# One hybrid decoder block on one core: the convolution's five VectorE operations three pieces apart and earlier, the merge's steps further apart, and decay's exponentials of odd chunks read straight from the running sums

## The chip, the cores and the metric

The kernel runs on one core of a Trainium2 chip as one launch. The metric is device time in microseconds (us), the median of several runs. A profiled execution gives the trace: PE is TensorE (PEld its weight loads), DVE is VectorE, ACT is ScalarE, POOL is GpSimd, SP is the engine that issues most DMAs. "L902" is line 902 of the kernel before.

## The reference, cut to what matters

```
proj = einsum('bsd,de->bse', rmsnorm(x), w_in)
(q, k, v, g_out, gk_low, gate_b, gate_c, xc, merge_a, merge_b) = split(proj)
log_g = log_sigmoid(gk_low @ w_gk_up + b_gk_up) / 16
bcum = cumsum(log_g, within chunks of 64 tokens)
q_dec, k_dec = q * exp(bcum), k * exp(-bcum)       # gated linear attention
o = rmsnorm(attention(q_dec, k_dec, v), gla_norm_w)
y_a = o * silu(g_out)
y_b = gate_b * causal_depthwise_conv(gate_c * xc, conv_w)   # three taps
merged = sigmoid(merge_a) * y_a + sigmoid(merge_b) * y_b
h = x + merged @ w_out
h = h + (silu(gate) * up) @ w_down                 # gate, up = rmsnorm(h) @ w_gate_up
return rmsnorm(h, final_norm_w)
```

There are 256 tokens, a model width of 2048, four heads and float32 throughout.

## The kernel before, in words

Every weight is streamed once, as 696 pieces of 128 x 1024 float32 (512 KB). The order of the pieces is a list written out ahead (`stream_list`). For each piece SP issues a DMA into `raw`, ScalarE makes a rounded copy `hi` (L238) and VectorE the rest `lo = raw - hi` (L243); TensorE then runs three matmuls for each product (L347 to L349). A whole product of four blocks ("eights") uses 12 matmuls of 512 columns for a piece. Some pairs of blocks (`gc`/`xc`, the gate and the input of the convolution) are computed as seven block products instead of eight ("sevens", 6 matmuls for a piece); they cost extra VectorE sums of whole pieces (L259 and L265, into the tiles `raw` and `x`).

The time of the program's own bookkeeping is the tick: one tick for each piece that TensorE uses up. `later(n, f)` puts `f` into the program n ticks on, `one_at_a_time(n, f)` at least n ticks on and two ticks after the one before. Pieces are prepared up to five ahead of TensorE (`LOOK`, and five buffers each for `raw` and `lo`). Instructions of each engine run in the order in which they stand on it; `pin` keeps some in the order of the program, the others may be moved by a scheduler. An engine that waits holds up all that stands behind on it.

The change touches two places.

**Decay.** `tables_within` builds an exponent table `eq` (128 x 8 x 256, four chunks of 64): chunks 0 and 2 get a difference (L750), chunks 1 and 3 a copy of the sums `bc` (L751). `exponential` (L738) makes two exponentials of it on ScalarE, `ek` and `eq`. `tables_across` does a similar thing on GpSimd for two more tables.

**Convolution and merge.** The gates come in four blocks i of 512 columns. When both `gc` and `xc` of block i are done, L954 multiplies them into `u`, and `conv(i)` one tick later shifts `u` by one and two tokens with six DMAs from GpSimd's queue (L889 to L894, into `u1` and `u2`; the taps were loaded long before). Five operations follow on VectorE (L902), pinned: `u1*tap1`, `u2*tap0`, `u*tap2`, `u1+u2`, `u+u1`, from tick `CONV_AT` = 12 on, one each tick. The first needs the three shifts into `u1`, the last of which is L893. `merge(i)` multiplies `u` into the gate (L907), adds `ya` a tick later (L908), and from three ticks on two sets of four transposes (`trb`, L595) go through TensorE, each of which ScalarE and VectorE copy out (L597, L598). Blocks 0, 1 and 2 run while the next pair's sevens are being multiplied; block 3 runs beside whole products only.

Of the kernel before, what the change touches and what calls it, by code (L numbers as in the profile page):

```python
# [11 lines left out]
AF = mybir.ActivationFunctionType  # L12
ALU = mybir.AluOpType
AX = mybir.AxisListType

P = 128
# [7 lines left out]
C = 64  # L24
# [160 lines left out]
def block_kernel(ctx, tc, x, xt, cols_in, gkw_in, gku_in, gnw, conv_w, finw, w_in, w_out, w_gu, w_dn, out):  # L185
    nc = tc.nc
    pin = tc.keep_in_program_order
# [11 lines left out]
    def bank(shape, name, tag=None):  # L199

        if tag is None:
            tag = f"b{turn['b'] % turn['of']}"
            turn["b"] += 1
        return psum.tile(shape, F32, tag=tag, name=name)
# [19 lines left out]
    count = {"loaded": 0, "used": 0, "tick": 0}  # L224
# [88 lines left out]
    def later(delay, fn):  # L313

        pending.append((count["tick"] + delay, fn))
# [15 lines left out]
    def one_at_a_time(delay, fn):  # L331

        spaced.append((count["tick"] + delay, fn))
# [256 lines left out]
    def transpose_block(src, t, hi, lo):  # L590

        lent.append(lent.pop(0))
        ps = bank([P, 4, P], "trb", lent[-1])
        for j in range(4):
            nc.tensor.transpose(out=ps[:, j, :], in_=src[:, j * P:(j + 1) * P], identity=ident)  # L595
        ts = slice(t * P, (t + 1) * P)
        nc.scalar.copy(hi[:, :, ts], ps)  # L597
        nc.vector.tensor_tensor(out=lo[:, :, ts], in0=ps, in1=hi[:, :, ts].bitcast(F32), op=ALU.subtract)  # L598
# [116 lines left out]
    inv = 1.0 / 16.0  # L715

    def ch(n):
        return bc[:, :, n * C:(n + 1) * C]

    def last(n):  # L720
        return bc[:, :, (n + 1) * C - 1:(n + 1) * C].to_broadcast([P, NM, C])
# [13 lines left out]

    first_exp = []

    def exponential(out, scale):  # L738

        ins = nc.scalar.activation(out, eq, AF.Exp, scale=scale)  # L740
        pin(ins)
        first_exp.append(ins.ins)

    def tables_within():
        nonlocal eq, ek
        eq = gpool.tile([P, NM, T], F32, tag="eq", name="eq")
        ek = gpool.tile([P, NM, T], F32, tag="ek", name="ek")

        for n in (0, 2):
            nc.vector.tensor_tensor(out=eq[:, :, n * C:(n + 1) * C], in0=ch(n), in1=last(n), op=ALU.subtract)  # L750
            nc.vector.tensor_copy(eq[:, :, (n + 1) * C:(n + 2) * C], ch(n + 1))  # L751
        exponential(ek, -inv)

    across = {}
# [1 line left out]
    def tables_across():  # L756

        exk = across["k"] = gpool.tile([P, NM, P], F32, tag="exk", name="exk")
        exq = across["q"] = gpool.tile([P, NM, P], F32, tag="exq", name="exq")
        nc.gpsimd.tensor_tensor(out=exk[:, :, 0:C], in0=last(0), in1=ch(0), op=ALU.subtract)  # L760
        nc.gpsimd.tensor_tensor(out=exk[:, :, 0:C], in0=exk[:, :, 0:C], in1=last(1), op=ALU.add)
        nc.gpsimd.tensor_tensor(out=exk[:, :, C:P], in0=last(1), in1=ch(1), op=ALU.subtract)
        nc.gpsimd.tensor_copy(exq[:, :, 0:C], ch(2))
        nc.gpsimd.tensor_tensor(out=exq[:, :, C:P], in0=ch(3), in1=last(2), op=ALU.add)
        with tc.issue_after(first_exp[-1]):
            nc.scalar.activation(exk, exk, AF.Exp, scale=inv)
            nc.scalar.activation(exq, exq, AF.Exp, scale=inv)

    def at(tick, fn):
        later(tick - count["tick"], fn)  # L770
# [6 lines left out]
    at(20, lambda: sum_decay(0))  # L777
    at(21, lambda: sum_decay(4))
    at(22, tables_within)
    at(23, lambda: exponential(eq, inv))  # L780
    at(25, tables_across)
    v_first = mm_first(gk_chunks, scale_rows)

# [42 lines left out]
    o = [omain.tile([P, NT, DV], F32, tag=f"m{i}", name="o") for i in range(H)]  # L826
# [51 lines left out]
    mh, ml = [None] * 4, [None] * 4  # L878
    us, ya, sb, merge_at = {}, {}, {}, {}

    def conv(i):
        u = us[i]
        u1 = ew.tile([P, NT, 512], F32, tag="u1", name="u1")
        u2 = ew.tile([P, NT, 512], F32, tag="u2", name="u2")
        taps = ew.tile([P, 3, 512], F32, tag="taps", name="taps")
        nc.gpsimd.dma_start(taps, conv_w[:, :, i * 512:(i + 1) * 512].to_broadcast([P, 3, 512]))
        nc.gpsimd.memset(u1[0:1, 0, :], 0.0)
        nc.gpsimd.memset(u2[0:2, 0, :], 0.0)
        nc.gpsimd.dma_start(u1[1:113, :, :], u[0:112, :, :])  # L889
        nc.gpsimd.dma_start(u2[2:114, :, :], u[0:112, :, :])  # L890
        nc.gpsimd.dma_start(u1[113:128, :, :], u[112:127, :, :])
        nc.gpsimd.dma_start(u2[114:128, :, :], u[112:126, :, :])
        nc.gpsimd.dma_start(u1[0:1, 1, :], u[127:128, 0, :])  # L893
        nc.gpsimd.dma_start(u2[0:2, 1, :], u[126:128, 0, :])  # L894

        def taps_of(j):
            return taps[:, j:j + 1, :].to_broadcast([P, NT, 512])

        for n, (dst, src, by, op) in enumerate(((u1, u1, 1, ALU.mult), (u2, u2, 0, ALU.mult), (u, u, 2, ALU.mult),
                                                (u1, u1, u2, ALU.add), (u, u, u1, ALU.add))):  # L900
            by = taps_of(by) if isinstance(by, int) else by
            later(CONV_AT + n, lambda d=dst, s=src, y=by, o=op: pin(nc.vector.tensor_tensor(out=d, in0=s, in1=y, op=o)))  # L902

    def merge(i, ts):

        v = sb[i][:, ts, :]
        pin(nc.vector.tensor_tensor(out=v, in0=v, in1=us[i][:, ts, :], op=ALU.mult))  # L907
        later(1, lambda: pin(nc.vector.tensor_tensor(out=v, in0=v, in1=ya[i][:, ts, :], op=ALU.add)))  # L908
        if mh[i] is None:
            mh[i] = omain.tile([P, 4, T], F32R, tag=f"m{i}", name="mh")  # L910
            ml[i] = oside.tile([P, 4, T], F32R, tag=f"m{i}", name="ml")
        for t in range(ts.start, ts.stop):
            one_at_a_time(3, lambda t=t: transpose_block(sb[i][:, t, :], t, mh[i], ml[i]))

    def gated(dst, ps):

# [4 lines left out]
    def gate(key):  # L921
        i = int(key[-1])

        def done(ps):
            if key[:-1] == "g":
                ya[i] = ew.tile([P, NT, 512], F32, tag=f"ya{i % 2}", name="ya")
                for t in range(NT):
                    nc.scalar.activation(ya[i][:, t, :], ps[t], AF.Silu, scale=r1[:, t:t + 1])
                nc.vector.tensor_tensor(out=ya[i], in0=ya[i], in1=o[i], op=ALU.mult)
            elif key[:-1] == "gb":  # L930
                sb[i] = ew.tile([P, NT, 512], F32, tag="sb", name="sb")
                for t in range(NT):
                    nc.scalar.activation(sb[i][:, t, :], ps[t], AF.Copy, scale=r1[:, t:t + 1])
            elif key[:-1] == "ma":
                gated(ya[i], ps)
            else:
                gated(sb[i], ps)

                at(max(count["tick"] + 1, merge_at.get(i, 0)), lambda: merge(i, slice(0, NT)))

        return done

    def gate_pair(pair):
        i = int(pair[0][-1])

        def second(t):
            to = us if pair[0][:-1] == "gc" else sb
            if i not in to:
                to[i] = ew.tile([P, NT, 512], F32, tag="u" if to is us else "sb", name="u" if to is us else "sb")
            return to[i][:, t, :]  # L950

        def done(t, one, two):
            if pair[0][:-1] == "gc":
                nc.vector.scalar_tensor_tensor(out=two, in0=one, scalar=r1sq[:, t:t + 1], in1=two,  # L954
                                               op0=ALU.mult, op1=ALU.mult)
                if t == 0:
                    later(1, lambda: conv(i))
                    merge_at[i] = count["tick"] + CONV_AT + 7
            else:
                nc.scalar.activation(two, two, AF.Sigmoid, scale=r1[:, t:t + 1])  # L960
                nc.vector.scalar_tensor_tensor(out=two, in0=one, scalar=r1[:, t:t + 1], in1=two,
                                               op0=ALU.mult, op1=ALU.mult)

                later(3 if t else 1, lambda: merge(i, slice(t, t + 1)))

        return second, done
# [191 lines left out]
    for e in order:  # L1158
        key, k0 = e
        n = int(key.split("_")[1])  # L1160
# [18 lines left out]
    assert not pending and not spaced and not ready and count["loaded"] == len(stream) + 1  # L1179


CONV_AT = 12
X_AT = (50, 54, 58, 62)
H_AT = (2, 4, 6, 8)
SQ_AT = (5, 7, 9, 11)
# [55 lines left out]
```

## Time and profile before

| what | value |
|---|---|
| median of 3 runs | 1503.78 us (1503.6, 1503.78, 1507.01) |
| the profiled execution | 1504.81 us, of which the span of its instructions is 1503.1 us |
| TensorE busy | 1489.7 us, 99% of the span, 7064 matmuls |
| VectorE busy | 1277.8 us, 85% |
| ScalarE busy | 864.1 us, 57% |
| granted TensorE clock | 0.999 of full speed |

A matmul of 512 columns is listed with 0.39 us because its end is modelled; the next one starts 0.23 us after it when nothing is waited for. So a wait of TensorE is read from the start of one matmul to the start of the next, less 0.227 us; the idle time that a row lists is 0.16 us shorter.

### The profile page before, as it was taken

The numbers are of one execution on the slowest core, as the hardware profiler recorded it, in microseconds if no ns is written. First come the engines' busy times: TensorE is split into PE (matmuls) and PEld (weight loads), VectorE is DVE, ScalarE is ACT, GpSimd is POOL, SyncE is SP. The second block draws the span as 40 slices with busy tenths as digits, with TensorE's granted clock in tenths as the row PEclk, the third lists the DMA queues.
The fourth block names the chain that finished last, engine by engine and source line by source line (L and its number), as shares of the span: only waits on it lengthen the run. The fifth ranks groups of instructions, "written<-read, shape, count | busy, mean of one in ns | idle before, by whom it ended". The sixth has DMA issues, their size and how long they took to land.

```text
span 1503.1 us, 19370 instructions
## 1 busy us (share of the span) xinstructions
PE 1489.7 (99%) x7064; PEld 1244.8 (83%) x7064; DVE 1277.8 (85%) x1283; ACT 864.1 (57%) x977; POOL 38.0 (3%) x60
## 2 busy tenths in 40 slices
PE   9999999999999999999999999999999999999997
PEld 8989988888887888888888888888888788888887
DVE  6785868979979878966689999999999999999975
ACT  7773546655655655654566755655565556565553
POOL 0030000000000000000000000000000000000000
PEclk9999999999999999999999999999999999999999
DMA  9656557876876878787677777776877788787782
GB/s 349 201 172 174 177 166 251 288 225 234 285 259 232 297 237 257 249 258 215 209 221 219 238 253 251 250 253 218 275 242 239 259 255 277 242 264 234 231 297 90
DMA packets 100128, 358.58 MB, mean 239 GB/s; under 512 B 11492, under 2 KB 11620, under 8 KB 99904
## 3 DMA queue, kind: packets, MB, share of 16 engines
q1 hardware_dynamic: 96656, 346.73, 70.8%
q0 software_dynamic: 2800, 8.89, 2.2%
q10 hardware_dynamic: 576, 1.72, 0.3%
q8 instruction: 55, 0.90, 0.2%
q14 instruction: 41, 0.34, 0.1%
HBM read 351.03 MB, written 2.10 MB: 235 GB/s over the span
## 4 chain that ended last, share of the span: by engine, by line
PE 53%; DVE 1%; issue 0%; ACT 0%; DVEq 0%; ACTq 0%
PE fg L347 8%; PE fg L349 8%; PE fg L348 8%; PE dn L347 5%; PE dn L349 5%; PE dn L348 5%; PE wo L347 2%; PE wo L348 2%; PE wo L349 2%; PE fu L349 1%; PE fu L347 1%; PE fu L348 1%; PE trb L595 1%; PE mb L349 0%; PE mb L348 0%
## 5 line engine op out<-in xcount | busy, mean ns | idle before, releaser
L243 DVE TENSOR_TENSOR lo<-raw,hi 128x1024 fp32r<-128x1024 f32 (+1 forms) x506 | 612.0, 1217 | 110.9 <-ACT hi L238 27.9
L238 ACT CAST hi<-raw 128x1024 fp32r<-128x1024 f32 (+1 forms) x506 | 523.9, 1047 | 269.9 <-PE gb L349 27.7
L238 ACT CAST hi<-x 128x1024 fp32r<-128x1024 f32 x144 | 151.7, 1053 | 267.4 <-DVE x L265 207.1
L243 DVE TENSOR_TENSOR lo<-x,hi 128x1024 fp32r<-128x1024 f32 x144 | 176.1, 1223 | 37.5 <-ACT hi L238 26.6
L347 PE MATMUL dn<-lo,acth 128*128 128x512 f32 (+1 forms) x368 | 140.7, 382 | 1.7 <-DVE h L1098 0.9
L349 PE MATMUL dn<-hi,acth 128*128 128x512 f32 (+1 forms) x368 | 139.9, 380 | 0.0
L348 PE MATMUL dn<-hi,actl 128*128 128x512 f32 (+1 forms) x368 | 139.9, 380 | 0.0
L265 DVE TENSOR_TENSOR x<-x,raw 128x1024 f32<-128x1024 f32 x96 | 117.0, 1218 | 12.0 <-DMA raw<-in_w_in_dram 7.7
L347 PE MATMUL fg<-lo,hh 128*128 128x512 f32 x288 | 112.4, 390 | 0.0
L349 PE MATMUL fg<-hi,hh 128*128 128x512 f32 x288 | 112.2, 390 | 0.0
L348 PE MATMUL fg<-hi,hl 128*128 128x512 f32 x288 | 112.2, 389 | 0.0
L347 PE MATMUL fg<-lo,sh 128*128 128x512 f32 x256 | 101.0, 395 | 0.0
L348 PE MATMUL fg<-hi,sl 128*128 128x512 f32 x256 | 99.9, 390 | 0.0
L349 PE MATMUL fg<-hi,sh 128*128 128x512 f32 x256 | 99.8, 390 | 0.0
L347 PEld LDWEIGHTS dn<-lo,acth 128*128 128x128 f32 x368 | 69.2, 188 | 15.8 <-DVE h L1098 1.8
L349 PEld LDWEIGHTS dn<-hi,acth 128*128 128x128 f32 x368 | 69.2, 188 | 13.3
L348 PEld LDWEIGHTS dn<-hi,actl 128*128 128x128 f32 x368 | 69.2, 188 | 12.9
L347 PEld LDWEIGHTS fg<-lo,hh 128*128 128x128 f32 x288 | 54.1, 188 | 11.8 <-DVE lo L243 0.5
L349 PEld LDWEIGHTS fg<-hi,hh 128*128 128x128 f32 x288 | 54.1, 188 | 11.3
L348 PEld LDWEIGHTS fg<-hi,hl 128*128 128x128 f32 x288 | 54.1, 188 | 11.0
L243 DVE TENSOR_TENSOR lo<-y,hi 128x1024 fp32r<-128x1024 f32 x48 | 58.5, 1218 | 4.8 <-ACT hi L238 2.1
L259 DVE TENSOR_TENSOR raw<-y,x 128x1024 f32<-128x1024 f32 x48 | 58.5, 1219 | 4.2 <-DMA y<-in_w_in_dram 3.3
(247 smaller groups left out, 3070.1 us busy)
## 6 DMA issues: line engine op xcount, KB each, us to landing
raw<-in_w_in_dram SPq DMA_DIRECT2D x254, 512.0 KB, 4.5
raw<-in_w_gu_dram SPq DMA_DIRECT2D x176, 512.0 KB, 4.4
raw<-in_w_dn_dram SPq DMA_DIRECT2D x88, 512.0 KB, 4.5
x<-in_w_gu_dram SPq DMA_DIRECT2D x32, 512.0 KB, 4.8
y<-in_w_gu_dram SPq DMA_DIRECT2D x32, 512.0 KB, 3.9
raw<-in_w_out_dram SPq DMA_DIRECT2D x32, 512.0 KB, 4.3
y<-in_w_in_dram SPq DMA_DIRECT2D x16, 512.0 KB, 4.4
x<-in_w_in_dram SPq DMA_DIRECT2D x16, 512.0 KB, 4.8
```

The source lines that it names most:

```text
L238: nc.scalar.copy(hi[:, ks, :], raw[:, ks, :])
L243: nc.vector.tensor_tensor(out=lo[:, ks, :], in0=raw[:, ks, :], in1=hi[:, ks, :].bitcast(F32), op=ALU.subtract)
L259: nc.vector.tensor_tensor(out=raw, in0=y, in1=held["x"], op=ALU.add)
L265: nc.vector.tensor_tensor(out=x, in0=x, in1=other, op=ALU.add)
L347: nc.tensor.matmul(ps, lhsT=sh, rhs=ml, start=first, stop=False, skip_group_check=onto)
L348: nc.tensor.matmul(ps, lhsT=sl, rhs=mh, start=False, stop=False, skip_group_check=onto)
L349: nc.tensor.matmul(ps, lhsT=sh, rhs=mh, start=False, stop=last, skip_group_check=onto)
L595: nc.tensor.transpose(out=ps[:, j, :], in_=src[:, j * P:(j + 1) * P], identity=ident)
```

## The change

The odd chunks are no longer copied into `eq` (two VectorE copies less) or `exq` (one GpSimd copy less); ScalarE reads them straight from `bc`, so two exponentials of 2048 elements become four of 1024, and one of 1024 becomes two of 512. The convolution's operations stand at ticks 6, 9, 12, 15, 18 for blocks 0 to 2 and 6, 8, 10, 12, 14 for block 3, in place of 12 to 16. The merge may begin 21 ticks (block 3: 17) after the point from which it was 19; its addition comes two ticks after its product, not one; the transposes come at least four ticks after, not three.

```diff
-        ins = nc.scalar.activation(out, eq, AF.Exp, scale=scale)
-        pin(ins)
+        for o, i in zip(halves(out), (halves(eq)[0], halves(bc)[1])):
+            ins = nc.scalar.activation(o, i, AF.Exp, scale=scale)
+            pin(ins)
...
             nc.vector.tensor_tensor(out=eq[:, :, n * C:(n + 1) * C], in0=ch(n), in1=last(n), op=ALU.subtract)
-            nc.vector.tensor_copy(eq[:, :, (n + 1) * C:(n + 2) * C], ch(n + 1))
...
-        nc.gpsimd.tensor_copy(exq[:, :, 0:C], ch(2))
...
-            nc.scalar.activation(exq, exq, AF.Exp, scale=inv)
+            nc.scalar.activation(exq[:, :, 0:C], ch(2), AF.Exp, scale=inv)
+            nc.scalar.activation(exq[:, :, C:P], exq[:, :, C:P], AF.Exp, scale=inv)
...
-            later(CONV_AT + n, lambda d=dst, s=src, y=by, o=op: pin(nc.vector.tensor_tensor(out=d, in0=s, in1=y, op=o)))
+            later(CONV_AT[i] + CONV_STEP[i] * n, lambda d=dst, s=src, y=by, o=op: pin(nc.vector.tensor_tensor(out=d, in0=s, in1=y, op=o)))
...
-        later(1, lambda: pin(nc.vector.tensor_tensor(out=v, in0=v, in1=ya[i][:, ts, :], op=ALU.add)))
+        later(2, lambda: pin(nc.vector.tensor_tensor(out=v, in0=v, in1=ya[i][:, ts, :], op=ALU.add)))
...
-            one_at_a_time(3, lambda t=t: transpose_block(sb[i][:, t, :], t, mh[i], ml[i]))
+            one_at_a_time(4, lambda t=t: transpose_block(sb[i][:, t, :], t, mh[i], ml[i]))
...
-                    merge_at[i] = count["tick"] + CONV_AT + 7
+                    merge_at[i] = count["tick"] + CONV_AT[i] + 4 * CONV_STEP[i] + 3
...
-CONV_AT = 12
+CONV_AT = (6, 6, 6, 6)
+CONV_STEP = (3, 3, 3, 2)
```

The order of instructions moves in three places that matter. Line numbers in the new kernel are 5 higher here: its L907 is the old L902 (convolution), its L912 and L913 the old L907 and L908 (merge), its L924 the old L919 (the sigmoid's product); in `lo<-raw,hi` and `lo<-x,hi` stand the pieces' splits.

**VectorE, block 1, the start of the convolution.** `u_3961` is the once shifted `u1`. Before, from the split of the piece `y` on:

```order
L243 TENSOR_TENSOR lo<-y,hi 128x1024
L265 TENSOR_TENSOR x<-x,raw 128x1024
L243 TENSOR_TENSOR lo<-raw,hi 128x1024 x2
L243 TENSOR_TENSOR lo<-x,hi 128x1024
L265 TENSOR_TENSOR x<-x,y 128x1024
L243 TENSOR_TENSOR lo<-raw,hi 128x1024
L243 TENSOR_TENSOR lo<-x,hi 128x1024
L902 TENSOR_TENSOR u_3961<-u_3961,taps 128x1024
```

Now, from the same split on:

```order
L243 TENSOR_TENSOR lo<-y,hi 128x1024
L907 TENSOR_TENSOR u_3961<-u_3961,taps 128x1024
L243 TENSOR_TENSOR lo<-raw,hi 128x1024
L265 TENSOR_TENSOR x<-x,raw 128x1024
L243 TENSOR_TENSOR lo<-raw,hi 128x1024
L907 TENSOR_TENSOR u_3962<-u_3962,taps 128x1024
L243 TENSOR_TENSOR lo<-x,hi 128x1024
L265 TENSOR_TENSOR x<-x,y 128x1024
```

The first operation on the shifted data stands seven instructions earlier, right behind that split. In block 0 it stands just ahead of the split of `y`, six splits earlier than before; in block 2 just ahead of a split of `x`, six splits earlier.

**VectorE, block 1, the merge.** `sb` is the gate that becomes the merged block. Before:

```order
L919 TENSOR_TENSOR sb<-sb,mb_0_4024 128x512
L919 TENSOR_TENSOR sb<-sb,mb_1_4025 128x512
L243 TENSOR_TENSOR lo<-x,hi 128x1024
L907 TENSOR_TENSOR sb<-sb,u 128x1024
L265 TENSOR_TENSOR x<-x,y 128x1024
L243 TENSOR_TENSOR lo<-raw,hi 128x1024
L908 TENSOR_TENSOR sb<-sb,ya 128x1024
L243 TENSOR_TENSOR lo<-x,hi 128x1024
L243 TENSOR_TENSOR lo<-raw,hi 128x1024
L265 TENSOR_TENSOR x<-x,raw 128x1024
```

Now:

```order
L243 TENSOR_TENSOR lo<-x,hi 128x1024
L924 TENSOR_TENSOR sb<-sb,mb_0_4024 128x512
L265 TENSOR_TENSOR x<-x,y 128x1024
L924 TENSOR_TENSOR sb<-sb,mb_1_4025 128x512
L243 TENSOR_TENSOR lo<-raw,hi 128x1024
L912 TENSOR_TENSOR sb<-sb,u 128x1024
L243 TENSOR_TENSOR lo<-x,hi 128x1024
L243 TENSOR_TENSOR lo<-raw,hi 128x1024
L265 TENSOR_TENSOR x<-x,raw 128x1024
L913 TENSOR_TENSOR sb<-sb,ya 128x1024
```

The addition of `ya`, for which the transposes wait, now stands behind three more instructions of the stream (two splits and a sum), and the product with `u` behind the split of `raw` that it stood ahead of. Block 0 moves in the same way; in block 2 this stretch stands as before.

**TensorE, block 1, the first set of transposes.** `g_0` and `g_1` are the two token halves of one piece of the gate `g`. Before, the transposes stand four matmuls into the piece:

```order
L349 MATMUL gc_3_3997<-hi,sh 128x512
L347 MATMUL g_0_4309<-lo,xh 128x512
L348 MATMUL g_0_4309<-hi,xl 128x512
L349 MATMUL g_0_4309<-hi,xh 128x512
L347 MATMUL g_0_4309<-lo,xh 128x512
L595 MATMUL trb<-ident,sb 128x128 x4
L348 MATMUL g_0_4309<-hi,xl 128x512
```

Now they stand at its end, after all twelve, and the next `gc` piece follows:

```order
L349 MATMUL g_0_4308<-hi,xh 128x512
L347 MATMUL g_1_4309<-lo,xh 128x512
L348 MATMUL g_1_4309<-hi,xl 128x512
L349 MATMUL g_1_4309<-hi,xh 128x512
L347 MATMUL g_1_4309<-lo,xh 128x512
L348 MATMUL g_1_4309<-hi,xl 128x512
L349 MATMUL g_1_4309<-hi,xh 128x512
L595 MATMUL trb<-ident,sb 128x128 x4
L347 MATMUL gc_2_3996<-lo,sh 128x512
```

So the transposes moved back by eight matmuls. In block 2 they moved by the same eight; in block 0 by 21, from five matmuls into a piece of `gc` to two matmuls into the second piece of `ma` after it (one matmul of that `gc` piece, twelve of `ma`, six of `gc` and two of `ma` lie between). In block 3 they stand where they stood.

## Rows read from the trace of the kernel before

**Rows 1.** The page's busy times: us, share of the span, instructions

```profile
PE 1489.7 (99%) x7064; PEld 1244.8 (83%) x7064; DVE 1277.8 (85%) x1283; ACT 864.1 (57%) x977; POOL 38.0 (3%) x60
```

**Rows 2.** TensorE's waits, whole span: total us, times, longest

```profile
PE dn L347 <- DVE h L1098: 0.9, 2, 0.5
PE trb L595 <- DVE sb L908: 0.9, 1, 0.9
...
PE g L347 <- DVE lo L243: 0.7, 1, 0.7
PE gc L347 <- DVE lo L243: 0.5, 1, 0.5
```

**Rows 3.** Windows 331:383, 437:482 and 543:611, their sum: us busy

```profile
sum 165.00, PE 162.86 PEld 133.34 DVE 152.31 ACT 86.27 POOL 14.96; mean PE 54.29 PEld 44.45 DVE 50.77 ACT 28.76 POOL 4.99
```

**Rows 4.** Timeline of TensorE at its waits: start us, us, instruction, [idle before]

```profile
372.79 0.39 PE L347 MATMUL gc<-lo,sh 128*128 128x512 f32 x1
373.01 0.39 PE L348 MATMUL gc<-hi,sl 128*128 128x512 f32 x1
373.46 0.63 PE L595 MATMUL trb<-ident,sb 128*128 128x128 f32 x4
...
381.25 0.39 PE L349 MATMUL ma<-hi,xh 128*128 128x512 f32 x1
382.11 0.50 PE L347 MATMUL gc<-lo,xh 128*128 128x512 f32 x1 [0.47 <-DVE lo L243]
...
478.57 0.39 PE L349 MATMUL gc<-hi,sh 128*128 128x512 f32 x1
479.69 0.50 PE L347 MATMUL g<-lo,xh 128*128 128x512 f32 x1 [0.72 <-DVE lo L243]
...
608.17 0.39 PE L347 MATMUL g<-lo,xh 128*128 128x512 f32 x1
609.45 0.66 PE L595 MATMUL trb<-ident,sb 128*128 128x128 f32 x4 [0.89 <-DVE sb L908]
```

**Rows 5.** Timeline of VectorE, blocks 0 to 2

```profile
341.39 1.22 DVE L243 TENSOR_TENSOR lo<-y,hi 128x1024 fp32r<-128x1024 f32 x1
...
449.63 1.23 DVE L265 TENSOR_TENSOR x<-x,raw 128x1024 f32<-128x1024 f32 x1 [2.42 <-DMA raw<-in_w_in_dram]
...
457.85 1.22 DVE L902 TENSOR_TENSOR u<-u,taps 128x1024 f32<-128x1024 f32 x1
...
479.55 1.22 DVE L908 TENSOR_TENSOR sb<-sb,ya 128x1024 f32<-128x1024 f32 x1
...
552.91 1.22 DVE L243 TENSOR_TENSOR lo<-x,hi 128x1024 fp32r<-128x1024 f32 x1 [1.34 <-PE gb L347]
...
608.18 1.22 DVE L908 TENSOR_TENSOR sb<-sb,ya 128x1024 f32<-128x1024 f32 x1
```

**Rows 6.** Timeline of GpSimd: the issue of L893, blocks 0, 1, 2

```profile
334.62 0.53 POOL L893 DMA_DIRECT2D u<-u  x1
...
439.91 0.51 POOL L893 DMA_DIRECT2D u<-u  x1
...
545.64 0.52 POOL L893 DMA_DIRECT2D u<-u  x1
```

**Rows 7.** DMA issues of the same three stretches, L893: KB, us to landing

```profile
u<-u POOLq DMA_DIRECT2D x1, 2.0 KB, 8.0
...
u<-u POOLq DMA_DIRECT2D x1, 2.0 KB, 8.6
...
u<-u POOLq DMA_DIRECT2D x1, 2.0 KB, 10.9
```

**Rows 8.** Timeline of TensorE, block 2: first use of the split at 552.91

```profile
562.62 0.39 PE L347 MATMUL gc<-lo,sh 128*128 128x512 f32 x1
```

**Rows 9.** Timelines around decay's exponentials

```profile
81.68 1.92 ACT L740 ACTIVATE ek<-eq 128x2048 f32<-128x2048 f32 x1
...
83.49 1.22 DVE L243 TENSOR_TENSOR lo<-raw,hi 128x1024 fp32r<-128x1024 f32 x1
...
91.46 0.39 PE L347 MATMUL v<-lo,xh 128*128 128x512 f32 x1
```

More of the change, by code (lines that the diff above doesn't have):

```diff
@@ L736, in block_kernel, with halves @@
     first_exp = []
+    def halves(tile):
+        v = tile.rearrange("p m (t n c) -> p m t n c", n=2, c=C)
+        return v[:, :, :, 0, :], v[:, :, :, 1, :]
     def exponential(out, scale):
-        ins = nc.scalar.activation(out, eq, AF.Exp, scale=scale)
-        pin(ins)
+        for o, i in zip(halves(out), (halves(eq)[0], halves(bc)[1])):
+            ins = nc.scalar.activation(o, i, AF.Exp, scale=scale)
+            pin(ins)
         first_exp.append(ins.ins)
```

## The prediction, made before the change was run

> **What bounds the kernel now.** I read the page's busy times first: TensorE is busy 99% of the span and VectorE 85% [rows 1]. The reader is to see that only what makes TensorE wait can move the time, so the next view is TensorE's waits [rows 2]. They are few and short, and three of them lie where the change does: transposes waiting for the merge's addition (L908) and two matmul rows waiting for a split (L243). None lies around decay's exponentials, and the waits of the down projection have no part in the change. The third view is the sum over the three stretches in which convolution and merge of blocks 0 to 2 run: VectorE is busy 152.31 of 165.00 us, 92% [rows 3]. There it is the engine that TensorE waits for, and being in order it has a debt that grows with each extra operation.
>
> The fourth view is TensorE's timeline at the waits [rows 4]. A matmul starts 0.22 to 0.23 us after the one before (372.79, 373.01); I use 0.227. What exceeds this is the wait. Block 0: transposes at 373.46 after 373.01, so 0.22; a split at 382.11 after 381.25, so 0.63. Block 1: a split at 479.69 after 478.57, so 0.89. Block 2: transposes at 609.45 after 608.17, so 1.05. Together 2.79 us. This is all that the change could give back by taking waits away, 0.19% of the time.
>
> **The change part by part.** The span is 1503.1 us, the profiled execution 1504.81 us; the sum is made against the latter. It is 1.03 us above the median of 1503.78, and I take that off at the end.
>
> *Decay.* Two VectorE copies and a GpSimd copy go; ScalarE makes four exponentials of half the size for two, and two for one, with a start more for each. No TensorE wait lies here. The old pair, 1.92 us each from 81.68, would end at about 85.5 [rows 9], and the halves cannot end before that by more than the copies that go, nor, if each cost as much as a whole one, after 89.4. One cast that stood ahead of the exponentials now stands behind them; I take 1.1 us for a cast, a little less than VectorE's 1.22 us for a tile of that size. The split that needs it stood at 83.49 and TensorE took it at 91.46 [rows 9]. Now it ends at about 85.5 + 1.1 + 1.22 = 87.8, in the bad bound at 91.7. So it is 3.6 us early, or 0.2 us late. The gain is nothing too: the copies were never on the path. I take 0. If that cover were gone, each us late would be a us.
>
> *Convolution, block 1.* The order puts the first operation right behind the split of `y`. Before, VectorE was idle there: 2.42 us up to 449.63, for a DMA [rows 5]. So it was free from 447.21. The last shift that the operation needs is issued at 439.91 [rows 6] and lands 8.6 us later [rows 7], at 448.5. VectorE waits for it, but in a hole that was there anyway, and this moves 1.1 us of work into the hole. From the first operation on there is no more idle time: before, from 457.85 to 479.55, 18 whole instructions and two of half size stand in 21.70 us [rows 5], which is 1.142 us for each of 19 units. Now 27 whole ones and two halves stand between the first operation and L908, with the first itself 29 units, 33.1 us. L908 starts at 448.5 + 33.1 = 481.6 and ends 1.22 us later, at 482.8. Without the old wait TensorE begins its piece of `g` at 478.57 + 0.227 = 478.80. The transposes now come after its twelve matmuls, at 481.52. They wait 1.3 us. The old wait for a split goes: the product that stood ahead of it (L907) now stands behind, and the hole gave 1.1 us, together more than 0.89. Block 1: 0.89 off, 1.3 on.
>
> *Block 0.* VectorE reaches the first operation at 341.39, where a split stood [rows 5]; the shift is issued at 334.62 and lands 8.0 us later, at 342.6 [rows 6, 7]. The 1.2 us between are lost, and there was no hole. Up to L908 there are now 30 units, 34.3 us. One split of `x` stands directly behind its own sum, with ScalarE's cast between: 1.1 us more. L908 starts at 378.0 and ends at 379.2. TensorE, freed of the two old waits and of transposes that have moved back, goes from 373.46 through 20 matmuls (twelve, six, two) to the transposes at 378.0. They wait 1.2 us. The split that TensorE awaited at 381.25 now stands ahead of both copies of transposes, and behind the new wait it is in time. Block 0: 0.85 off, 1.2 on.
>
> *Block 2.* VectorE was free from 551.57 (552.91 less 1.34 us idle) [rows 5]. The shift lands 10.9 us after 545.64, at 556.5 [rows 6, 7]. So the first operation holds VectorE for 4.9 us, behind it a split that ends at 556.5 + 1.14 + 1.22 = 558.9. TensorE takes that split at 562.62 [rows 8], 3.7 us later, so it hides this. The weight DMAs that wait for VectorE's buffers go out late and the stretch runs up to 2 us behind for a while; later idle time should absorb most. The merge stands as it did, L908 ending at 609.40, but the transposes stand eight matmuls later: at 608.17 + 0.227 + 8 x 0.227 = 610.2, not 608.4. Up to 0.8 us of lateness costs nothing; 2 us would cost 1.2. I take 0. Block 2: 1.05 off, nothing on, at worst 1.2.
>
> *Block 3* has only whole products beside it, no wait in it and its transposes where they stood: 0.
>
> *Sum.* Off: 0.85 + 0.89 + 1.05 = 2.79. On: 1.2 + 1.3 + 0 = 2.5. Net -0.3: 1504.81 becomes 1504.5, and less 1.03 the median is 1503.5 us. The bounds: 2.79 off and nothing on is 1501.0; block 2's 1.2 on as well is 1504.7.
>
> *A rule weighed against the rows.* The rows say that the last shift lands 8.0, 8.6 and 10.9 us after its issue [rows 7], while the stream's own DMAs run. The Trainium skill, "DMA: Bandwidth & Descriptors", section "Anatomy of one DMA — SWDGE (gpsimd) path", fits about 2 us plus the bytes over 436 GB/s for such a DMA, an estimate of 4.4 us for all six shifts together; by it no first operation would wait. By that rule the sum would be 1.2 us lower (block 0), by the rows it stands; the rows are this kernel's and decide. The same page's section "Rules for kernel authors" advises issuing a DMA early and waiting for it late; it speaks against moving the first operation six ticks nearer to its shifts, and the trace's 1.2 and 4.9 us agree.
>
> **The rivals.** *All four waits go, nothing takes their place.* For it: VectorE has holes of 2.42 and 1.34 us ahead of the old convolution [rows 5] that earlier operations can fill. Against it: L908 stands behind three more instructions. It would need L908 1.3 us sooner than summed in both blocks. 1504.81 - 2.79 - 1.03 = 1501.0.
>
> *Slower: the shifts land later.* In blocks 0 and 1 VectorE has nothing idle between the first operation and L908, so each us that the last shift is late goes whole into the transposes' wait. With block 2's 10.9 us in both, that is 2.9 and 2.3 us more: -0.3 + 5.2 = +4.9, 1508.7. It counts as slower from 4.5 us over, that is from about 10.7 us in both. For it: the spread of 8.0 to 10.9. Against it: block 2's came under a denser stretch, and ahead of the first operation of block 0 nothing has changed.
>
> *The shifts are there in time* (the rule above, as a mechanism: a first operation that finds its data). Block 0 gains its 1.2 us; block 1 nothing, since what follows waits for the DMA at 449.63 all the same. 1502.3. Against it stand all three rows.
>
> *The change does nothing that TensorE sees*, the new waits being just the old: 1503.8. It is hardly to be told from the forecast.
>
> **How the numbers follow.** Two measurements of this kernel can be told apart from about 0.3%, 4.5 us. My forecast, new waits about as long as the old, gets 0.52; no change 0.1; all waits gone 0.16; shifts in time 0.08; shifts later 0.14, of which 0.05 is beyond 4.5 us. No case is faster by 4.5 us, since all waits together are 2.79; 0.04 is kept for what I have not seen. Slower gets 0.05 and 0.01 for the same reason. The range goes from the case without waits, 1501.0, to 3 us of later shifts, 1506.5.
>
> **What would show it.** In the changed profile: TensorE's waits should have no more row of `gc` or `g` for a split in blocks 0 and 1, and L908's successor should hold the transposes 1.2 us in block 0 and 1.3 in block 1, and not at all in block 2. VectorE's first convolution operation should be listed as waiting for GpSimd's shifts, about 1 us in blocks 0 and 1 and 4 to 5 us in block 2. Around decay no wait of TensorE may appear. I am wrong if transposes wait nowhere, if a wait of TensorE appears in block 2, or if VectorE has idle time between the first operation and the merge's addition in blocks 0 and 1.

## The result, and the profile after

The changed kernel takes 1510.06 us, the kernel before 1504.73 us (medians of 11 runs each); the ratio is 1.0031, 95% interval 1.0019 to 1.0043. By this ratio it is about 4.7 us slower (the two medians lie 5.3 us apart), and every one of its runs (1507.5 to 1515.19) lies above the 1506.5 us at which my range ended. The profiled execution took 1507.51 us, nearly the fastest of the eleven; its span is 1505.8 us, 2.7 us longer than before.

The page's busy times hardly move against [rows 1]:

```profile
PE 1489.5 (99%) x7064; PEld 1244.3 (83%) x7064; DVE 1276.9 (85%) x1281; ACT 863.4 (57%) x980; POOL 35.6 (2%) x59
```

TensorE's waits over the whole span, to be held against [rows 2] (total us, times, longest):

```profile
PE trb L595 <- DVE sb L913: 2.6, 1, 2.6
PE dn L347 <- DVE h L1103: 1.5, 3, 0.6
...
PE trb L595 <- issue: 1.0, 1, 1.0
PE dn L347 <- DVE lo L243: 0.8, 1, 0.8
PE ma L347 <- ACT ya L933: 0.6, 1, 0.6
```

The waits of `g` and `gc` for a split are gone, as forecast. Three rows took their place. TensorE's timeline puts them in the program; it answers to [rows 4]:

```profile
369.98 0.39 PE L349 MATMUL ma<-hi,xh 128*128 128x512 f32 x1
370.94 0.50 PE L347 MATMUL ma<-lo,xh 128*128 128x512 f32 x1 [0.58 <-ACT ya L933]
...
378.11 0.39 PE L348 MATMUL ma<-hi,xl 128*128 128x512 f32 x1
379.48 0.63 PE L595 MATMUL trb<-ident,sb 128*128 128x128 f32 x4 [0.98 <-issue]
...
482.11 0.39 PE L349 MATMUL g<-hi,xh 128*128 128x512 f32 x1
485.12 0.66 PE L595 MATMUL trb<-ident,sb 128*128 128x128 f32 x4 [2.63 <-DVE sb L913]
```

From start to start, less 0.227 us, the waits are 0.74 and 1.14 us in block 0 and 2.79 us in block 1 (in nanoseconds; these rows are rounded); block 2 has none. Instead of 2.79 us in the three blocks TensorE now waits 4.67 us, 1.9 more. The row "issue" names no releaser; the timeline of VectorE shows that the addition ended just ahead of the transposes, at 379.27. That timeline, to be held against [rows 5]:

```profile
341.85 1.23 DVE L907 TENSOR_TENSOR u<-u,taps 128x1024 f32<-128x1024 f32 x1 [0.91 <-DMA u<-u]
...
365.55 1.23 DVE L265 TENSOR_TENSOR x<-x,raw 128x1024 f32<-128x1024 f32 x1 [0.75 <-DMA raw<-in_w_in_dram]
...
378.05 1.22 DVE L913 TENSOR_TENSOR sb<-sb,ya 128x1024 f32<-128x1024 f32 x1
...
449.26 1.23 DVE L907 TENSOR_TENSOR u<-u,taps 128x1024 f32<-128x1024 f32 x1 [1.27 <-DMA u<-u]
...
471.29 1.23 DVE L265 TENSOR_TENSOR x<-x,raw 128x1024 f32<-128x1024 f32 x1 [1.22 <-DMA raw<-in_w_in_dram]
...
483.85 1.22 DVE L913 TENSOR_TENSOR sb<-sb,ya 128x1024 f32<-128x1024 f32 x1
...
558.17 1.23 DVE L907 TENSOR_TENSOR u<-u,taps 128x1024 f32<-128x1024 f32 x1 [3.94 <-DMA u<-u]
```

VectorE waits for the shifts, as forecast. But in blocks 0 and 1 it waits a second time, between the first operation and the addition, for a piece `raw`: 0.75 and 1.22 us. I had written that nothing idles there, but for 1.1 us of a cast in block 0 (measured 1.20). GpSimd's and SP's timelines show what goes out just ahead of that piece in block 1, and the DMA issues of the same stretch (461 to 462.5 us) how long both take (KB, us to landing):

```profile
461.28 0.81 POOL L891 DMA_DIRECT2D taps<-in_conv_w_dram  x1 [19.56 <-DVE u L907]
...
462.15 0.33 SPq L232 DMA_DIRECT2D raw<-in_w_in_dram  x1
```

```profile
taps<-in_conv_w_dram POOLq DMA_DIRECT2D x1, 768.0 KB, 9.1
raw<-in_w_in_dram SPq DMA_DIRECT2D x1, 512.0 KB, 9.1
```

These are the taps of the next block. They go into the tile that the convolution's third operation is the last to read, so they start as soon as that operation is over. The change put it from tick 14 to tick 12, and the transfer of 768 KB moved with it, from 465.04 in the kernel before to 461.28, to just ahead of a piece that VectorE soon needs. GpSimd's timeline and the DMA issue in the kernel before:

```profile
465.04 0.81 POOL L886 DMA_DIRECT2D taps<-in_conv_w_dram  x1 [24.11 <-DVE u L902]
```

```profile
taps<-in_conv_w_dram POOLq DMA_DIRECT2D x1, 768.0 KB, 11.0
```

There the transfer was no faster, and pieces issued beside it took 7.7 and 10.4 us, but VectorE waited for none of them.

### The profile page after: what moved, and what is told of

Read it like the earlier page. It is cut to its first block, busy times and chain, and to the rows that moved or that the text cites. A ratio compares the mean times of both kernels' runs of the same rounds, so it can differ in the third digit from the quotient of the medians.

```text
span 1505.8 us, 19372 instructions
## 1 busy us (share of the span) xinstructions
PE 1489.5 (99%) x7064; PEld 1244.3 (83%) x7064; DVE 1276.9 (85%) x1281; ACT 863.4 (57%) x980; POOL 35.6 (2%) x59
## 3 DMA queue, kind: packets, MB, share of 16 engines
q10 hardware_dynamic: 576, 1.72, 0.3%
## 4 chain that ended last, share of the span: by engine, by line
PE 89%; DVE 3%; DMA 2%; issue 2%; ACT 2%; SPq 0%; DVEq 0%; ACTq 0%
PE fg L349 7%; PE fg L347 7%; PE fg L348 7%; PE dn L347 4%; PE dn L349 4%; PE dn L348 4%; PE gc L347 3%; PE gc L349 3%; PE gc L348 3%; PE gb L347 2%; PE v L348 2%; PE v L347 2%; PE v L349 2%; PE gb L349 2%; PE gb L348 2%
## 5 line engine op out<-in xcount | busy, mean ns | idle before, releaser
L265 DVE TENSOR_TENSOR x<-x,raw 128x1024 f32<-128x1024 f32 x96 | 117.1, 1220 | 8.8 <-DMA raw<-in_w_in_dram 4.4
```

What stands on the lines that cost most here:

```text
L265: nc.vector.tensor_tensor(out=x, in0=x, in1=other, op=ALU.add)
```

## The experiments

All ratios are to the kernel before, with the 95% interval; medians are of 9 to 12 runs (e3: 5). "Waits" are TensorE's in the stretches of blocks 0, 1 and 2 (330 to 437, 437 to 545, 545 to 670 us) of the one profiled execution, worked out from matmul starts as above, all that exceed 0.15 us.

| kernel | median us | ratio | waits, us |
|---|---|---|---|
| before | 1504.73 | 1 | 0.85, 0.89, 1.05 |
| changed | 1510.06 | 1.0031 (1.0019 to 1.0043) | 1.88, 2.79, 0 |
| e1 changed, again | 1508.71 | 1.0022 (1.0013 to 1.0031) | 1.72, 4.17, 0 |
| e2 decay alone | 1504.22 | 0.9991 (0.9982 to 0.9999) | 0.87, 0, 1.38 |
| e3 convolution alone | 1510.86 | 1.0035 (1.0023 to 1.0048) | 2.21, 2.79, 1.91 |
| e4 changed, late taps | 1505.51 | 1.0000 (0.9991 to 1.001) | 1.45, 1.82, 0 |
| e5 merge alone | 1505.4 | 1.0005 (0.9996 to 1.0013) | 0.39, 3.46, 0 |
| e6 before, late taps | 1503.77 | 0.999 (0.9982 to 0.9999) | 0.85, 0.25, 0.75 |
| e7 no hold, taps as before | 1505.79 | 1.0002 (0.9994 to 1.0011) | 1.28, 2.47, 0 |
| e8 late taps and transposes | 1508.93 | 1.0024 (1.0013 to 1.0035) | 1.91, 4.07, 0 |
| e9 no hold, early taps | 1507.54 | 1.0018 (1.0007 to 1.0029) | 2.29, 2.83, 0 |
| e10 no hold, late taps | 1505.6 | 1.0003 (0.9995 to 1.0012) | 1.36, 1.83, 0 |
| e11 mixed | 1504.33 | 0.9994 (0.9986 to 1.0003) | 0.86, 1.24, 0 |
| e12 changed, a third time | 1509.3 | one run | 2.11, 3.59, 0 |

The medians of before in the four groups of runs were 1504.73, 1505.89 (for e1 to e4), 1504.98 (e5 to e8) and 1505.11 (e9 to e12). The kernels whose waits add up to more than 4.5 us (changed, e1, e3, e8, e9) are those whose whole interval lies above 1. Below that, sum and ratio follow each other only loosely (e5: 3.85 us and 1.0005).

### Which part of the change costs (e2, e3, e5)

e2 leaves convolution and merge as before; e3 takes only the ticks of the convolution, with decay as before and `later(1, ...)` and `one_at_a_time(3, ...)` in the merge; e5 takes only the merge's spread:

```diff
-        later(1, lambda: pin(... in1=ya[i][:, ts, :], op=ALU.add)))
+        later(2 if i < 3 else 1, lambda: pin(... in1=ya[i][:, ts, :], op=ALU.add)))
-            one_at_a_time(3, lambda t=t: transpose_block(...))
+            one_at_a_time(4 if i < 3 else 3, lambda t=t: transpose_block(...))
```

> Only decay's exponentials are changed; convolution and merge as before. Theory A: nothing, 1504.7 within 1 us, and the waits of before in blocks 0 to 2 (0.85, 0.89, 1.05 us). Rival B: 2 us or more slower than before.

> Only the convolution's operations stand at the new ticks; the merge's addition comes one tick and the transposes three ticks on, as before, decay as before. Theory A: VectorE waits for the shifts and for the late piece as in the changed kernel, so it is 1 to 5 us slower than before, with waits of the transposes or of splits in blocks 0 and 1. Rival C (the merge's spread, which puts the addition three instructions further back, is what costs): no slower than before by 1 us, 1503.5 to 1505.5.

> Only the merge is spread in blocks 0 to 2: its addition two ticks behind its product, the transposes at least four ticks on; convolution, block 3 and decay as before. Theory A (the shifts and the earlier taps cost, the spread does not): no slower than before; as the waits of 0.22, 0.9 and 1.05 us stand ahead of steps that now come later, 0 to 1.5 us faster, 1503.5 to 1505.5. Rival C: 2 us or more slower.

The convolution alone costs as much as the whole change, 1.0035. The merge's spread alone costs nothing that can be told, so rival C falls. Decay costs nothing, so rival B falls; whether it gains is open (below). In block 2 of e3 the transposes, which stand earlier there than in the changed kernel, wait too (1.38 us). In block 1 e3 has the same wait of VectorE for the late piece:

```profile
470.80 1.23 DVE L265 TENSOR_TENSOR x<-x,raw 128x1024 f32<-128x1024 f32 x1 [1.10 <-DMA raw<-in_w_in_dram]
```

### Taps or hold (e4, e7, e9, e10)

Two things come with the new ticks: the hold of VectorE for the shifts, and the earlier taps. These four runs take away one, the other, or both. e4 and e10 load the next taps only behind the merge's addition, through a GpSimd copy of one element that the transfer has to follow:

```diff
+    def load_taps(i, after=None):
+        taps = ew.tile([P, 3, 512], F32, tag="taps", name="taps")
+        if after is not None:
+            nc.gpsimd.tensor_copy(taps[0:1, 0, 0:1], after[0:1, 0, 0:1])
+        nc.gpsimd.dma_start(taps, conv_w[:, :, i * 512:(i + 1) * 512].to_broadcast([P, 3, 512]))
...
+        if i < 3:
+            later(2, lambda: load_taps(i + 1, v))
```

e7 and e10 start later, with the third operation at tick 14 as before; e9 starts later too, but keeps the third at tick 12:

```diff
-CONV_AT = (6, 6, 6, 6)
-CONV_STEP = (3, 3, 3, 2)
+CONV_AT = (10, 10, 10, 6)
+CONV_STEP = (2, 2, 2, 2)
```

```diff
-            later(CONV_AT[i] + CONV_STEP[i] * n, lambda ...)
+            later((10, 11, 12, 15, 18)[n] if i < 3 else 6 + 2 * n, lambda ...)
```

> The changed kernel, with the next block's taps loaded only behind the merge's addition and no longer behind the third operation of the convolution; the order on VectorE, ScalarE and TensorE is the same. Theory A: the pieces that landed late beside the taps (8.6 to 8.8 us after issue, blocks 0 and 1) land in about 5 us, VectorE's waits of 0.75 and 1.22 us behind the first operation go, the transposes of block 1 wait about 1.5 us and not 2.8, and the median is 2 to 3 us below the changed kernel's: 1507.5. If the taps' transfer has no part in it (rival D: the pieces land late because the shifts hold VectorE and so the buffers): as the changed kernel, 1509 to 1511.

> The changed kernel, with the convolution's five operations of blocks 0 to 2 at ticks 10, 12, 14, 16, 18 in place of 6, 9, 12, 15, 18: the last operation and the merge's earliest tick stay, the first finds its shifts landed, and the third, which lets the next taps go, stands at tick 14 as before. Theory A: VectorE's waits for shifts go and the late pieces return to what they were before; the transposes' waits in blocks 0 and 1 shrink by 1 us or more each, 1505.5 to 1507. If the hold for the shifts were without price (rival E: what VectorE loses there it would lose a little later to the stream anyway) and the taps' earlier place the whole cost: 1505 to 1506.5 too, but in the trace a wait of VectorE for a piece takes the place of that for the shifts, ahead of the first operation.

> The changed kernel, with the operations of blocks 0 to 2 at ticks 10, 11, 12, 15, 18: the first finds its shifts landed, but the third, behind which the next taps are loaded, stays at tick 12. Theory A (the earlier taps are the cost): as the changed kernel, 1508.5 to 1510, with VectorE waiting about 1 us for a late piece in blocks 0 and 1. Rival G (hold and early taps cost only together, since the hold uses up the lead by which late pieces are caught up): as before, 1504.5 to 1506.5, and no wait for a late piece, or one that TensorE does not see.

> The changed kernel with both taken away: operations of blocks 0 to 2 at ticks 10, 12, 14, 16, 18 and the next taps loaded behind the merge's addition. Theory A and rival G: no better than with one of them away, 1504 to 1506, since what is left is the addition that stands further back, about 1 us in block 0 and 1.7 in block 1. If hold and taps each have their own price, which add up: 2 us or more below, 1502 to 1503.5.

In e4 VectorE, ScalarE and TensorE run the same order as in the changed kernel, the hold for the shifts is still there (1.35 and 1.60 us in blocks 0 and 1), and the slowdown is gone (1505.51 us; 1507.5 were forecast). VectorE's timeline of e4, the first operation of blocks 0 and 1 and the addition of block 1:

```profile
342.91 1.22 DVE L916 TENSOR_TENSOR u<-u,taps 128x1024 f32<-128x1024 f32 x1 [1.35 <-DMA u<-u]
...
449.77 1.23 DVE L916 TENSOR_TENSOR u<-u,taps 128x1024 f32<-128x1024 f32 x1 [1.60 <-DMA u<-u]
...
483.04 1.22 DVE L922 TENSOR_TENSOR sb<-sb,ya 128x1024 f32<-128x1024 f32 x1
```

Between first operation and addition VectorE waits for no piece in either block. The piece that took 9.1 us takes 3.5, by the DMA issues around its issue at 462.65:

```profile
raw<-in_w_in_dram SPq DMA_DIRECT2D x1, 512.0 KB, 3.5
```

So rival D falls: the piece was not late because the hold kept its buffer, since here the hold is as long. The transposes of block 1 wait 1.82 us and not 2.79. In e9 there is no hold, the taps stay early, and more than half of the slowdown stays: 1.0018 (1507.54 us, 1 us below the range that theory A gave). VectorE's timeline of e9:

```profile
363.68 1.23 DVE L265 TENSOR_TENSOR x<-x,raw 128x1024 f32<-128x1024 f32 x1 [0.88 <-DMA raw<-in_w_in_dram]
...
450.31 1.23 DVE L265 TENSOR_TENSOR x<-x,raw 128x1024 f32<-128x1024 f32 x1 [2.24 <-DMA raw<-in_w_in_dram]
...
471.84 1.23 DVE L265 TENSOR_TENSOR x<-x,raw 128x1024 f32<-128x1024 f32 x1 [1.00 <-DMA raw<-in_w_in_dram]
```

The late pieces are there without a hold, so rival G (hold and taps cost only together) falls. The middle row is the hole of the kernel before [rows 5], which the early first operation had filled: rival E is right that what the hold takes in block 1 would be lost to the stream anyway. With the third operation two ticks later (e7) the taps go out at 464.95, behind the piece in question, and VectorE waits for no piece between first operation and addition in these two blocks. What is left of TensorE's waits in e7 lies at the transposes (0.48 and 1.73 us) and at gates behind them (0.81 and 0.74 us). That piece and the taps, by the DMA issues of e7 at 460.1 and 464.95:

```profile
raw<-in_w_in_dram SPq DMA_DIRECT2D x1, 512.0 KB, 3.7
...
taps<-in_conv_w_dram POOLq DMA_DIRECT2D x1, 768.0 KB, 8.8
```

e10, with neither, is no better than e4 or e7. The earlier taps are the cost. With late taps the hold has no price that can be measured (e4 against e10); with early taps the intervals of e9 and of the changed kernel overlap, so whether the hold adds something there stays open.

### Where else the debt can go (e8, e6, e11)

e8 is e4 with the transposes of blocks 0 to 2 two ticks further back (`one_at_a_time(6 if i < 3 else 4, ...)`). e6 is the kernel before with late taps. e11 has the changed decay, late taps, and the new ticks and spread in block 2 alone (`CONV_AT = (12, 12, 6, 12)`, `CONV_STEP = (1, 1, 3, 1)`).

> The changed kernel with the taps loaded behind the merge's addition and the transposes of blocks 0 to 2 at least six ticks behind the merge's product and not four; nothing else moves but the copies out of the transposes. Theory A (what is left of the new waits is that the addition ends after TensorE has come to the transposes, 1.14 and 1.82 us with late taps alone): both waits go, no other takes their place, 2.5 to 3 us below late taps alone, 1502.5 to 1503.5, faster than before. If VectorE is behind as a whole (rival F), TensorE waits for a split instead and it is less than 1 us below late taps alone: 1504.5 to 1505.5.

> The kernel before, with only the next block's taps loaded behind the merge's addition; the order on VectorE, ScalarE and TensorE is that of before. Theory A with a wider reach (the taps' transfer costs the kernel before too, since pieces issued beside it land 7.7 to 11.1 us after issue): the waits for a split in blocks 0 and 1 (0.63 and 0.89 us) go, 1 to 1.5 us faster than before, about 1504. Narrow theory (before, VectorE has enough other work while these pieces land, so the taps only cost once they are moved forward): as before, within 0.7 us.

> The best of what has been seen: decay changed; convolution and merge as before in blocks 0, 1 and 3 and as changed in block 2, where TensorE waited 1.05 us before and nothing after; the next taps behind the merge's addition. If the parts add up: the 1.4 us of decay alone, the 1.5 us of late taps in the kernel before (both not far beyond their intervals) and up to 1.05 us of block 2, so 2 to 4 us below before, 1501 to 1503. If decay's and the taps' are one and the same chance difference in block 1's wait: 1 to 1.5 us below.

e8 missed both ways: neither faster nor equal, but 1.0024. The waits of the transposes did go, and others came at 406 and 511 us. Timelines of TensorE and ScalarE at the second:

```profile
507.00 1.05 ACT L238 CAST hi<-raw 128x1024 fp32r<-128x1024 f32 x1 [2.25 <-DMA raw<-in_w_in_dram]
...
514.23 0.50 PE L347 MATMUL ma<-lo,xh 128*128 128x512 f32 x1 [2.51 <-ACT ya L944]
```

TensorE waits for the activation of a gate on ScalarE (`ya`), which stands behind casts, one of which waited 2.25 us for a piece. In e8 the taps load from 489.41 to 500.81 us. The piece issued beside them at 490.83 lands 9.5 us later, and the one that the cast waits for, issued at 499.63, lands 7.3 us later. Rival F was nearer, though the wait is not for a split: as I read it, TensorE ran ahead by what it no longer waited and met the late pieces further on. No run here moves the taps within e8, so this is not shown. The clock fell there too, as in e1 below.

e6 and e11 are the only ones besides e2 whose ratio is below 1, by about 1.5 and 0.9 us. e6's interval ends just under 1, e11's includes it. In e6 the wait in block 1 went as expected and that in block 0 stayed. The parts do not add up in e11: its block 1 waits 0.97 us for a split, although both e2 and e6 had lost that wait. I take no version here to be shown faster than the kernel before.

### More profiles of the changed kernel (e1, e12)

> The changed kernel once more, for a second profiled execution. Theory A: the time went into TensorE's waits for the transposes in blocks 0 and 1 (1.14 and 2.79 us in the first profile), because VectorE loses time between the first convolution operation and the merge's addition: it waits for the shifts (0.91 and 1.27 us) and later for a piece `raw` that lands late (0.75 and 1.22 us), beside the transfer of the next block's taps. Then the median is about 1510, and in this profile the same two transposes wait, each by at least what VectorE waits for shifts and pieces there, whatever the single sizes are; a longer execution has longer waits there. Rival B (the decay part disturbs the whole program): the waits of the transposes are alike and the difference lies elsewhere.

> The changed kernel a third time, for a profile. Theory A: the transposes wait 1.1 to 1.3 us in block 0 and 2.6 to 2.9 us in block 1, where VectorE waits about 1 us for a late piece both times. In the second profile the granted clock fell to half behind the wait in block 1, which cost 1.35 us, and in the first it did not; if it falls here too, that is what makes most executions longer than the first profiled one.

The same places wait in all three profiled executions: the transposes 1.14, 1.18 and 1.14 us in block 0 and 2.79, 2.70 and 2.24 us in block 1, with VectorE waiting 0.55 to 0.88 and 1.07 to 1.22 us for the late pieces. The sizes do not follow what I expected: e1's wait in block 1 is shorter than the first profile's though its execution is longer, and e12's 2.24 us lies below the range of 2.6 to 2.9. The second and third have something more behind the wait in block 1. Windows of e1 (length in us; busy time and count of PE, PEld, DVE, ACT and POOL; granted clock, DMA share, GB/s):

```profile
482.00:485.30 3.30, 0.76 (x4) 0.63 (x4) 3.30 (x4) 1.72 (x2) 0.00 (x0) 0.90 0.71 221
485.30:487.60 2.30, 2.30 (x8) 1.91 (x7) 2.30 (x3) 2.30 (x4) 0.00 (x0) 0.50 0.61 216
```

and TensorE's timeline there:

```profile
484.67 1.12 PE L595 MATMUL trb<-ident,sb 128*128 128x128 f32 x4 [2.54 <-DVE sb L913]
...
486.44 0.63 PE L349 MATMUL gc<-hi,sh 128*128 128x512 f32 x1
486.86 0.63 PE L347 MATMUL gc<-lo,sh 128*128 128x512 f32 x1
487.29 0.63 PE L348 MATMUL gc<-hi,sl 128*128 128x512 f32 x1
```

For 2.3 us matmuls start 0.43 us apart and not 0.227: the clock is at the lower of its two levels, 1.2 of 2.4 GHz. It fell in e12 as well, but whether this makes most executions longer than the first profiled one is not settled: over whole runs the granted clock is 0.999 in the one of 1510.06 us and 0.998 both in the longest (1515.19) and in the first profiled one (1507.51).

## Why the prediction was wrong

The step that failed is in block 1: "From the first operation on there is no more idle time". I took it from the kernel before, where 18 whole instructions and two halves ran back to back, and asked of the new order only what VectorE computes. The third operation issues no DMA itself, but one waits for it, that of the taps (L886 of the kernel before). I had dismissed it as "loaded long before", which holds for the block's own taps and not for the next block's, which use the same tile. Where the prediction had no idle time, the runs showed VectorE idle for 1.22 us at a piece that landed late beside these taps. The prediction had named such idle time as a sign of being wrong. e4 moves this transfer alone (with a GpSimd copy of one element) and gives the loss back; e9 keeps it and keeps more than half of the loss. Point by point:

- **Block 1.** Forecast 1.3 us of wait, measured 2.79. The addition was to start 0.1 us after TensorE came to the transposes (481.6 against 481.52, then 1.22 us long); it started 1.5 us after (483.85 against 482.34), and 1.22 us of this is the wait for the piece. From the start of the first operation to that of the addition I had 33.1 us. It took 34.59 us in the changed kernel and 33.27 in e4, so the sum over VectorE's work was right and the late piece was the term that it lacked. The hold at the first operation was as forecast (until 449.26; 448.5 forecast, with everything some 0.8 us later by then), and mostly in the old hole.
- **Block 0.** Forecast 1.2, measured 1.14 us at the transposes, but not by my chain alone. There too a piece was late, by 0.75 us, and with it a sum (L265), a cast behind it on ScalarE and the gate `ya` behind that cast, for which TensorE's `ma` waited 0.74 us. TensorE came to the transposes that much later, so the two nearly cancelled there, and the 0.74 us came on top. Late taps bring that wait to 0.31 us in e4 and leave 1.14 us at the transposes.
- **Block 2.** Right: VectorE was held 3.94 us (4.9 forecast), TensorE did not see it, and the old wait of 1.05 us is gone.
- **Decay.** Right: there is no wait of TensorE from 70 to 130 us. The split that I had ending at 87.8 ended at 87.89; TensorE took it at 90.92, 3.0 us later. That the number fits is luck: the exponentials ended at 84.36, 1.1 us sooner than I had them, and VectorE's own work kept the split from starting before 86.67. e2 alone is 0.9991, with an interval that just excludes 1; since the wait that is missing in its block 1 (0.89 us) is back in e11 with the same decay, I don't settle whether this is a gain of the part.
- **Rivals.** "The shifts land later" had the right consequence (each us that VectorE loses between first operation and addition goes whole into the transposes' wait) and the wrong transfer: the shifts land 7.6 to 9.8 us after issue, no later than before, and the hold has no price that e4 and e10 show. e4 bears the consequence out: there VectorE loses 1.32 us less behind the first operation and 0.33 us more at it, and the transposes of block 1 wait 0.97 us less. The chances of the five cases already add up to 1, so the 0.04 and 0.01 kept for the unseen came on top of them. I had weighed one transfer and missed the one that the moved operation lets go.
- **The rule.** The Trainium skill, "DMA: Bandwidth & Descriptors", section "Anatomy of one DMA — SWDGE (gpsimd) path", gives by its fit an estimate of 3.8 us for the 768 KB of taps (2 us and the bytes over 436 GB/s). This case's transfer took 9.1 us beside the stream, and the piece beside it 9.1 instead of 3.5; the measurements decide, as they did for the shifts.
- **The sum.** Forecast -0.3 us; the first profile's blocks give +1.9, e1's +3.1 (5.89 less 2.79), clock included, e12's +2.9. With late taps, which is the change as I had pictured it, the sum is 3.27 us against 2.79, and the measured ratio 1.0000. By the ratios the change costs 3.3 us (0.22%, e1) and 4.7 us (0.31%). e1's blocks nearly cover the first. In the first profile 1.0 us more of the span's 2.7 lies behind 1100 us, where TensorE's waits, mostly of the down projection, come to 2.2 us before, 3.1 to 3.3 us in the three profiles of the changed kernel and 2.4 to 5.1 us in the others. Some 2 us of the 4.7 are in no profile and are left open.

## What to carry to other kernels

When an operation moves, list what it frees as well as what it needs: a transfer that waits for the last reader of a tile moves with that reader. Then look which transfers are issued just behind it, and whether an engine without slack waits for one of them; here 768 KB of taps, four microseconds earlier, cost more than all the waits that the change removed. And a wait taken away at one place can come back at another: in e8 those at the transposes went, and longer ones came at the gates.

## What the runs showed of the hardware

Beside a broadcast load of 768 KB from GpSimd's queue, the first four pieces of 512 KB issued behind it on SP's queue landed 7.1 to 9.3 us after issue (changed kernel, block 1); the same four pieces landed after 3.5 to 4.4 us in e4, where the load comes later. What each queue had of the DMA engines from 461.3 to 470.4 us, the time of the taps' transfer, in the changed kernel (packets, MB, share of the time of 16 engines; q0 is GpSimd's queue, q1 SP's):

```profile
q0 software_dynamic: 208, 0.79, 56.2%
q1 hardware_dynamic: 306, 1.12, 31.1%
```

and in e4:

```profile
q1 hardware_dynamic: 590, 2.15, 71.9%
```

The taps took more than half of the engines' time for 0.79 MB, and the stream moved about half as much as without them. The Trainium skill, "DMA: Bandwidth & Descriptors", section "Queues, rings and completion order", says that each DMA engine goes round the queues that have work, a packet at a time; the trace agrees that both queues move together, and its numbers say what that costs here.

After waits of TensorE of 2.2 to 2.8 us the granted clock fell to 1.2 GHz in some executions and not in others. In e1 it was 0.50 from 485.3 to 487.6 us, behind an idle time of 2.54 us, and in e12 0.51 from 486 to 489 us, behind 2.08 us. In e8 seven matmuls ran at the lower level behind 2.51 us. In e3 the clock stayed at 1.00 behind 2.62 us, and so it did in the first profile of the changed kernel behind 2.63 us, as this window shows:

```profile
485.00:487.30 2.30, 2.18 (x12) 1.88 (x13) 2.30 (x4) 2.30 (x4) 0.00 (x0) 1.00 0.89 253
```

Each matmul of 512 columns at the lower level starts 0.2 us late (the first 0.35 us in e1 and e12). In all that is 1.3 us in e1 and e12 and 1.4 us in e8, behind waits of 2.70, 2.24 and 2.67 us, so such a wait cost about half as much again as it lasted.
